# One decoder layer on one core: where the down product of five of eight expert waves stands

## The chip, the cores and the metric

The kernel runs on one core of a Trainium2 chip. The metric is the device time of one execution in microseconds (us). A run of the kernel before took 1399.57 us (median of three, 1397.91 to 1399.74). Tensor products run on TensorE (PE in the profile), elementwise work on VectorE (DVE), ScalarE (ACT) and GpSimd (POOL); SyncE (SP) issues the weight loads.

## The reference, cut to what matters

256 tokens of width 2048 pass one layer in float32: a convolution and an attention group, an output projection, a mixture of experts, and a gated layer embedding. What the change touches is the last two:

```
h = h + HierMoE(rms_norm(h))          # 32 experts, each token goes to two of them
    per expert e:  hidden = silu(xb @ w_gate[e]) * (xb @ w_up[e])     # 2048 -> 512, twice
                   y      = (hidden @ w_down[e]) * weight of the token  # 512 -> 2048
    out = sum of y by token
gate = sigmoid(rms_norm(h) @ w_ple_gate)                               # 2048 -> 2048
h = h + gate * (p @ w_ple)
```

The weights w_gate, w_up and w_down hold 32 x 2048 x 512 float32 each, 134 million bytes; all weights must be read once, 484 million bytes in all with inputs and outputs.

## The kernel before, in words

The order of all instructions on each engine is the order in which the program writes them. SBUF has 24 slots of 8 KB per partition (the tile tag "ring"), shared by the weight loads and the large buffers. The list `loads` fixes the order in which the weights are read; `pump` (L64) issues the next loads from it, on SP's queue (L74), whenever fewer than 24 slots less the reserved ones are in use, and `free` (L78) gives a slot back behind the instruction that read it last. Nearly every load is 1 MB, one slot.

The first stage (until about 385 us) makes the input projection, convolution, attention, output projection and routing. The 32 experts then run in eight waves of four, with 32 token slots an expert, so that a wave fills the 128 columns of the array's output side by side.

`gate_up(w)` (L949) multiplies the gathered tokens of a wave with its gate and up weights, 128 products of 512 columns in eight groups of four loads. After the third quarter it gathers the tokens of the next wave (`gather`, L933, products at L938). At its end it makes silu(gate) * up, transposes it (L990) and leaves it in SBUF (`hTw`). A gate or up load has 8 KB in one piece in HBM for each partition.

Only when all eight waves are through does the down product begin, by chunks of output columns (`TC`, L138): three of 512 columns and two of 256. For a chunk, `down_waves` (L1058) goes through the waves: `down_wave` (L1038, products at L1047) makes the outputs of a wave's four experts by slot in one PSUM bank, ScalarE copies them (L1064), and `scatter` (L1052, L1054) sums them by token, with the weights of the routing, into the tile `po`, which holds the chunk's sum of all waves for both halves of the tokens. `add_down` (L1070) adds it to the residual. A load of w_down is [128, 4, 512] or [128, 8, 256]: pieces of 2 KB or 1 KB.

Each finished chunk of columns is also a part of the contraction of the gate product. `gate_product(ci)` (L1138) runs in the background of the next chunk: every call of `bg` takes it one step on, and `down_waves` calls `bg` once behind each wave (`per=1`). Its first call transposes the chunk (`rows`, L1093), then each step splits a piece of gate weights in two parts (ScalarE L336, VectorE L337) and makes 12 products of 512 columns (L1128 to L1130). Of a 512 column chunk there are eight steps: four blocks of 512 output columns, two steps each; behind the second step of a block its two PSUM halves are copied or added to `gs` in SBUF (L1154 on ScalarE for chunk 0, L1156 on VectorE for later ones). The PSUM pool "pa" has two tiles of two banks: one holds `po` during a chunk, the other the block of the gate product. `drain` takes all steps that are left, ahead of the chunk's last wave. Of a 256 column chunk there are four steps, and their blocks alternate between a "pa" tile and two "ps" banks.

The loads follow the same order: gate and up of all waves, then for each chunk w_down of all waves and the chunk's gate weights. The last chunk ends with the norm's scale, the last gate steps, the sigmoid and the output.

Of the kernel before, what the change touches and what calls it, by code (L numbers as in the profile page):

```python
# [22 lines left out]
NW = NE // 4  # L23
NSLOT = 24
NEG_D = -1e30


@with_exitstack
def kernel(ctx: ExitStack, tc: tile.TileContext, I, out):
# [15 lines left out]

# [1 line left out]
    used, KEEP = [0], [0]  # L47

    def reserve(n):
        KEEP[0] += n  # L50
# [39 lines left out]

# [1 line left out]
    w_in_v = w_in.rearrange("(k p) n -> p k n", p=128)  # L92
# [39 lines left out]
    def want_d(w, c0, n):  # L132
        m = 512 // n
        for e in range(4 * w, 4 * w + 4, m):
            want(("d", e, c0), [128, 4 * m, n],
                 w_down[e:e + m].rearrange("e (j p) n -> p (e j) n", p=128)[:, :, c0:c0 + n])

    TC = [(0, 512), (512, 512), (1024, 512), (1536, 256), (1792, 256)]  # L138
    for w in range(NW):
        want_gu(w)  # L140
        if w == 5:
            want("p", [128, 2, 256], p.rearrange("(t p) k -> p t k", p=128))
            for k in range(2):
                want(("ple", k), [128, 2048], w_ple[128 * k:128 * k + 128, :])
    w_pg_v = w_pg.rearrange("(k p) n -> p k n", p=128)

    def pg_units(c0, cn):
        """first column and width of the loads of a chunk's gate weights"""
        if (c0, cn) == TC[-1]:
            return [(0, 512), (512, 512), (1024, 1024)]  # L150
        return [(n0, 2048 * 128 // cn) for n0 in range(0, D, 2048 * 128 // cn)]
# [8 lines left out]

    for c0, cn in TC[:3]:
        for w in range(NW):
            want_d(w, c0, cn)
        want_pgs(c0, cn)
    for c0, cn in TC[3:]:
        for w in range(NW):
            if w == NW - 1:
                want_pgs(c0, cn, 0)
            want_d(w, c0, cn)
        want_pgs(c0, cn, 1, 2) if cn == 256 else None  # L170

# [1 line left out]
    xs = [alloc([128, 4, 512], F32R, f"xs{i}") for i in range(4)]  # L173
# [47 lines left out]
    for s in range(2):  # L221
        nc.gpsimd.memset(onesbd[64 * s:64 * s + 64, 64 * s:64 * s + 64], 1.0)
    # a column of ones for each head
    hsel = kvt[:, 1920:2048]
    nc.gpsimd.memset(hsel, 0.0)
    for s in range(2):
        nc.gpsimd.memset(hsel[64 * s:64 * s + 64, s:128:18], 1.0)
    # -(distance) of a key from its query, far below zero outside the window
    nc.gpsimd.iota(dist[:, 0:128], pattern=[[1, 128]], base=0, channel_multiplier=-1,
# [26 lines left out]

# [2 lines left out]
    ss4 = C.tile([128, 2, 4], F32, name="ss4")  # L259
# [27 lines left out]
    def token_rows(pt, xrow, n):  # L287
        """adds a value by token to every row of pt"""
        for b in range(n):
            for tt in range(2):  # L290
                c0 = 256 * b + 128 * tt
                nc.tensor.matmul(pt[:, c0:c0 + 128], xrow[:, tt], ident, start=n == 1 and tt == 0,
                                 stop=b == n - 1 and tt == 1, skip_group_check=True)
# [32 lines left out]

# [1 line left out]
    granules = [("in", name, hf, q) for name, _, hf in units for q in range(2)]  # L328
# [24 lines left out]
    def keep_warm(n):  # L353
        """matmuls on constants, that the tensor engine's clock isn't gated while it waits"""
        for _ in range(n):
            nc.tensor.matmul(ps(), ident, wr.rearrange("p k n -> p (k n)")[:, 0:512], start=True, stop=True)
# [23 lines left out]

# [1 line left out]
    def halves(pt, dst):  # L382
# [38 lines left out]
    def q_sums(u):  # L421
        """sums of squares by token and head; the heads' scale goes on the scores"""
        sq = w2([128, 2, 256], "sq")
        q = qT[:, 2 * u:2 * u + 2, :]
        nc.gpsimd.tensor_mul(sq, q, q)
        yield
        yield
        if u == 0:
            prq[0] = ps()
        for b in range(2):  # L430
            h = 2 * u + b
            nc.tensor.matmul(prq[0][0:16, 0:256], hsel[:, 16 * h:16 * h + 16], sq[:, b],
                             start=h == 0, stop=h == 7)
        yield
        if u == 3:
            qs = w2([16, 256], "qs")
            nc.scalar.copy(qs, prq[0][0:16, 0:256])
            yield
            pv = ps()[:, 0:32].rearrange("p (t h) -> p t h", t=2)
            for tt in range(2):  # L440
                nc.tensor.transpose(pv[:, tt], qs[:, 128 * tt:128 * tt + 128], ident[0:16, 0:16])
            yield
            for tt in range(2):
                nc.scalar.activation(rq[:, tt], pv[:, tt], AF.Sqrt, bias=epsn[:, tt:tt + 1], scale=1.0 / HD)
            nc.vector.reciprocal(rq, rq)
            nc.vector.tensor_mul(rq, rq, slope[:, 1, None, :].to_broadcast([128, 2, NH]))
# [107 lines left out]
    def mixed(kb, y, sacc, gcol, eng):  # L554
        """two blocks of a head group's output: their squares, and their parts for the projection"""
        sq = w2([128, 2, 256], "sq")
# [56 lines left out]

# [1 line left out]
    rac = C.tile([128, 2, 2], F32, name="rac")  # L615
# [19 lines left out]
    def last_group(i, pt):  # L635
        """the last two granules: the first 128 tokens before the second, and those in two halves of the
        columns, so that the router's work on a part runs beside the products of the next"""
        hT = w2([128, 4, 128], "hT"), w2([128, 4, 128], "hT")
# [185 lines left out]

# [1 line left out]
    rt = C.tile([128, 2, 8], F32, name="rt")  # L826
# [12 lines left out]

    # the group: the first of the largest logits  # L840
    nc.vector.tensor_reduce(gm, Lg, axis=AX.X, op=OP.max)
# [3 lines left out]
    for tt in range(2):  # L845
# [4 lines left out]
                            gt[:, :, 12:16, None].to_broadcast([128, 2, NG, EPG]), op=OP.add)  # L850
    # its two experts: those above the second largest logit, then the first of those equal to it
    for tt in range(2):
# [16 lines left out]
    nc.tensor.matmul(pr2[:, 0:32], tri[:, 0], asg[:, 1], start=False, stop=True)  # L869
    # rank of a token among those of its expert, from 1 on; 0 where it isn't assigned  # L870
    for tt, pp in ((0, pr_), (1, pr2)):
# [14 lines left out]

    # assignments past an expert's slots, for the general path at the end
    cnt = C.tile([128, 32], F32, name="cnt")
# [12 lines left out]

# [1 line left out]
    xg, sel = {}, {}  # L903
# [45 lines left out]
    def gate_up(w):  # L949
# [4 lines left out]
        for j4 in range(4):  # L954
            if j4 == 0 and w == NW - 1:
                reserve(6)
            for n, nm in enumerate("gu"):
# [33 lines left out]
        nc.scalar.copy(hTw(w), p2)  # L991

    ple = [None, None]

# [26 lines left out]
    for w in range(NW):  # L1021
        gate_up(w)
        if w == 1:
            overflow_counts()
        if w == 4:
            reserve(3)
        if w == 5:
            ple_product()

# [1 line left out]
    acc = hmid  # L1031
    gs = [alloc([128, D], F32, "gs") for _ in range(2)]
    wsl[:] = [alloc([128, 2048], F32R, f"wsq{i}") for i in range(3)]
# [4 lines left out]
    def down_wave(w, c0, cn):  # L1038
        """the outputs of a wave's experts, by slot"""
        m = 512 // cn  # L1040
# [11 lines left out]
    def scatter(po, w, y, off, cn):  # L1052
        for tt in range(2):
            nc.tensor.matmul(po[:, tt, off:off + cn], swT(w)[:, 128 * tt:128 * tt + 128], y,  # L1054
                             start=w == 0 and (tt == 0 or cn == 512 or ci < last),
                             stop=w == NW - 1, skip_group_check=True)
# [36 lines left out]
    def rows(ci):  # L1093
        """the columns of a chunk, transposed, with the norm's gain, split in two parts"""
        c0, cn = TC[ci]
# [64 lines left out]
    for ci in range(last):  # L1160
        po = pa()
        prev = down_waves(po, range(NW - 1), *TC[ci], 0)
        drain()
# [9 lines left out]
    po = ps().rearrange("p (t n) -> p t n", t=2)  # L1173
    prev = down_waves(po, range(NW - 2), c0, cn, 0)
    drain()
# [55 lines left out]

# [1 line left out]
    def overflow():  # L1233
# [126 lines left out]
```

## Time and profile before

| | |
|---|---|
| runs, median (lowest, highest) | 1399.57 us (1397.91, 1399.74) |
| profiled execution: span | 1398.5 us, 1.07 us below the median of the runs |
| TensorE products (PE) busy | 1160.8 us, 83% |
| VectorE, ScalarE, POOL busy | 360.3, 265.2, 133.1 us |
| granted clock, mean | 0.937 |
| moved | 484.32 MB, mean 346 GB/s |
| chain that ended last | DMA 49%, PE 37%, DVE 5%, ACT 3%, SP's queue 3% |

The profile has one execution. Busy times are unions, so matmuls that overlap count once, but a product that waits for the end of its group's loads counts as busy. The span in 40 slices has one slice per 35 us. "idle before <-X" says how long an engine stood idle and what ended it.

### The profile page before, as it was taken

Reading aid. Unit: us, or ns where it says so; the run is one execution under the profiler, and the core shown is the slowest. Engines: PE = TensorE matmul, PEld = TensorE weight load, DVE = VectorE, ACT = ScalarE, POOL = GpSimd, SP = SyncE. Lnnn points to the kernel's source line nnn. Section 1 sums busy time; section 2 is a strip of 40 time slices with the busy share of each in tenths; the row PEclk is TensorE's granted clock in tenths of the full one; section 3 lists DMA queues with packets and bytes.
Section 4 is the critical chain, followed back from the end, with each engine's and each line's share of the span. In section 5 each row is a group of like instructions: output and inputs, shape, how many; then the busy total and the mean of one; then the engine's idle time right before and its main releaser. Section 6 shows DMA issues by size and latency. Waiting matters only on the chain.

```text
span 1398.5 us, 15423 instructions
## 1 busy us (share of the span) xinstructions
PE 1160.8 (83%) x6411; PEld 644.8 (46%) x6412; DVE 360.3 (26%) x535; ACT 265.2 (19%) x456; POOL 133.1 (10%) x157
## 2 busy tenths in 40 slices
PE   7999999999996967778687887866686886996996
PEld 6878777888751513224151431511111441443654
DVE  5747887555300000101010000100000211212325
ACT  5435555443100000000000010000000211111213
POOL 2215566000000000000000000000000000000002
PEclk9999999999998999999999898998998997997999
DMA  8972247976899999999999999999999999999993
GB/s 241 344 246 86 66 147 251 337 224 229 316 410 422 421 421 421 421 421 421 422 421 421 419 421 421 420 422 406 387 387 387 365 387 378 359 387 354 357 350 138
DMA packets 181638, 484.32 MB, mean 346 GB/s; under 512 B 7940, under 2 KB 78012, under 8 KB 149564
## 3 DMA queue, kind: packets, MB, share of 16 engines
q1 hardware_dynamic: 180572, 480.59, 90.6%
q0 software_dynamic: 992, 2.69, 0.6%
q8 instruction: 52, 0.85, 0.2%
q14 instruction: 22, 0.18, 0.0%
HBM read 478.80 MB, written 4.19 MB: 345 GB/s over the span
## 4 chain that ended last, share of the span: by engine, by line
DMA 49%; PE 37%; DVE 5%; ACT 3%; SPq 3%; issue 1%; POOL 1%; DVEq 0%; ACTq 0%
DMA ld<-in_w_up_dram 36%; DMA ld<-in_w_down_dram 12%; PE pst L1047 6%; PE pat L758 5%; PE pst L938 3%; SPq L74 3%; PE pat L759 3%; PE pat L963 3%; PE pat L736 2%; PE pat L738 2%; PE pat L737 2%; PE pat L1054 2%; PE pat L1129 1%; PE pat L1130 1%; PE pat L1128 1%
## 5 line engine op out<-in xcount | busy, mean ns | idle before, releaser
L963 PE MATMUL pat<-ld,xg 128*32 128x512 f32 x2048 | 340.7, 675 | 117.5 <-DMA ld<-in_w_up_dram 69.8
L963 PEld LDWEIGHTS pat<-ld,xg 128*32 128x32 f32 x2048 | 79.9, 120 | 363.9 <-issue 147.4
L1047 PE MATMUL pst<-ld,wv 128*32 128x512 f32 (+1 forms) x1280 | 169.4, 551 | 58.0 <-DMA ld<-in_w_down_dram 57.9
L758 PE MATMUL pat<-xs,wsp 128*128 128x512 f32 x544 | 196.3, 404 | 0.0
L759 PE MATMUL pat<-xs,wsp 128*128 128x256 f32 x544 | 153.1, 281 | 0.7 <-DVE wsp L337 0.7
L337 DVE TENSOR_TENSOR wsp<-ld,wsp 128x1024 fp32r<-128x1024 f32 x91 | 131.2, 1447 | 82.9 <-ACT wsp L336 82.9
L940 DVE TENSOR_TENSOR xg<-pst,gffn 128x512 f32<-128x512 f32 (+1 forms) x33 | 22.3, 675 | 438.4 <-PE pst L938 438.4
L336 ACT CAST wsp<-ld 128x1024 fp32r<-128x1024 f32 x104 | 108.0, 1049 | 91.7 <-PE pat L738 44.0
L1047 PEld LDWEIGHTS pst<-ld,wv 128*32 128x32 f32 x1280 | 45.6, 115 | 171.3 <-issue 87.5
L938 PEld LDWEIGHTS pst<-sel,x 128*128 128x128 f32 x512 | 112.6, 311 | 9.8 <-issue 8.1
L758 PEld LDWEIGHTS pat<-xs,wsp 128*128 128x128 f32 x544 | 103.2, 190 | 27.9 <-issue 2.8
L938 PE MATMUL pst<-sel,x 128*128 128x128 f32 x512 | 114.7, 384 | 0.0
L759 PEld LDWEIGHTS pat<-xs,wsp 128*128 128x128 f32 x544 | 103.7, 191 | 1.3 <-DVE wsp L337 1.3
L947 ACT COPY wv<-pst 128x256 f32<-128x256 f32 x8 | 3.0, 374 | 440.9 <-PE pst L946 440.9
L1064 ACT COPY y<-pst 128x512 f32<-128x512 f32 (+1 forms) x40 | 20.0, 501 | 306.6 <-PE pst L1047 306.6
L337 DVE TENSOR_TENSOR wsq<-ld,wsq 128x1024 fp32r<-128x1024 f32 x32 | 39.1, 1224 | 136.5 <-ACT wsq L336 136.5
L1128 PE MATMUL pat<-wsq,hs 128*128 128x512 f32 x112 | 53.4, 476 | 12.9 <-ACT wsq L336 11.8
L1054 PE MATMUL pat<-y,wv 128*128 128x512 f32 (+1 forms) x128 | 55.6, 562 | 0.0
L336 POOL CAST wsq<-ld 128x1024 fp32r<-128x1024 f32 x1 | 1.0, 1042 | 558.2 <-DVE x L1072 558.2
L736 PE MATMUL pat<-wsp,mx 128*128 128x512 f32 (+1 forms) x128 | 49.8, 389 | 0.1
L738 PE MATMUL pat<-wsp,mx 128*128 128x512 f32 (+1 forms) x128 | 49.0, 383 | 0.0
L931 POOL TENSOR_TENSOR sel<-sel,et 128x128 f32<-128x128 f32 x16 | 6.1, 400 | 451.3 <-DVE sel L929 357.5
(269 smaller groups left out, 1005.5 us busy)
## 6 DMA issues: line engine op xcount, KB each, us to landing
ld<-in_w_gate_dram SPq DMA_DIRECT2D x128, 1024.0 KB, 19.8
ld<-in_w_up_dram SPq DMA_DIRECT2D x128, 1024.0 KB, 19.8
ld<-in_w_down_dram SPq DMA_DIRECT2D x128, 1024.0 KB, 14.1
ld<-in_w_in_dram SPq DMA_DIRECT2D x35, 1024.0 KB, 12.6
ld<-in_w_out_dram SPq DMA_DIRECT2D x16, 1024.0 KB, 10.7
ld<-in_w_ple_gate_dram SPq DMA_DIRECT2D x15, 1024.0 KB, 14.3
x<-in_x_dram SPq DMA_DIRECT2D x8, 256.0 KB, 6.7
spill<-x POOLq DMA_DIRECT2D x8, 256.0 KB, 5.9
```

The costliest lines, as they stand in the source:

```text
L74: nc.sync.dma_start(t[:, i] if isinstance(src, list) else t, part)
L336: copy(t[:, :, 0], src)
L337: eng.tensor_sub(t[:, :, 1], src, t[:, :, 0].bitcast(F32))
L736: nc.tensor.matmul(o, mh, ws[:, kk, 0, cs], start=first, stop=False)
L738: nc.tensor.matmul(o, ml, ws[:, kk, 0, cs], start=False, stop=last)
L758: nc.tensor.matmul(pt[:, b, :], ws[:, kk, 0, bs], xk, start=first, stop=False)
L759: nc.tensor.matmul(pt[:, b, 0:256], ws[:, kk, 1, bs], xk[:, 0:256], start=False, stop=last)
L938: nc.tensor.matmul(pt[:, 128 * jj:128 * jj + 128], hmid[tt][:, j::16], sel[w][:, tt], start=tt == 0, stop=tt == 1)
L963: nc.tensor.matmul(pt[32 * e:32 * e + 32, n, :], g[:, j, 32 * e:32 * e + 32], wt, start=j == 0, stop=j == 15, tile_position=(0, 32 * e))
L1047: nc.tensor.matmul(pt[32 * e:32 * e + 32, 0:cn], hv[:, j, 32 * e:32 * e + 32], d, start=j == 0, stop=j == 3, tile_position=(0, 32 * e))
L1054: nc.tensor.matmul(po[:, tt, off:off + cn], swT(w)[:, 128 * tt:128 * tt + 128], y, start=w == 0 and (tt == 0 or cn == 512 or ci < last), s ...
L1128: nc.tensor.matmul(pt[tt], mh, ws[:, kk, 0], start=start and b == 0, stop=False)
```

## The change

A constant `NROW = 5` is added. For waves 0 to 4 the loads of w_down move from the chunks to the place behind the wave's gate and up loads, and are whole rows, [128, 2048], 16 of 1 MB per wave. A new function `down_rows` runs directly behind `gate_up` for these waves: 64 products into four PSUM banks, four copies, eight scatter products, and eight additions (for the first wave copies) on VectorE into two new SBUF buffers `macc`, which hold the sum by token. Behind the last wave the two sums are added to the residual, and the buffers become `gs`. The chunks keep waves 5 to 7; `bg` is called three times behind each of waves 5 and 6 (in the last chunk twice behind wave 5). A few reservations of slots change with the two buffers; comment lines are dropped.

```diff
+NROW = 5
@@
+    def want_rows(w):
+        for j in range(4):
+            for e in range(4 * w, 4 * w + 4):
+                want(("r", e, j), [128, D], w_down[e, 128 * j:128 * j + 128, :])
@@
     for w in range(NW):
         want_gu(w)
+        if w < NROW:
+            want_rows(w)
@@
     for c0, cn in TC[:3]:
-        for w in range(NW):
+        for w in range(NROW, NW):
             want_d(w, c0, cn)
         want_pgs(c0, cn)
     for c0, cn in TC[3:]:
-        for w in range(NW):
+        for w in range(NROW, NW):
@@ gate_up
             if j4 == 0 and w == NW - 1:
-                reserve(6)
+                reserve(4)
@@
+    macc = [None, None]
+
+    def down_rows(w):
+
+        hv = hTw(w).rearrange("p (j s) -> p j s", j=4)
+        pts = [ps() for _ in range(4)]
+        for j in range(4):
+            for n in range(4):
+                for e in range(4):
+                    nc.tensor.matmul(pts[n][32 * e:32 * e + 32, :], hv[:, j, 32 * e:32 * e + 32],
+                                     arrived["r", 4 * w + e, j][:, 512 * n:512 * n + 512],
+                                     start=j == 0, stop=j == 3, tile_position=(0, 32 * e))
+            free(4)
+        ys = []
+        for n in range(4):
+            y = w2([128, 512], "y")
+            nc.scalar.copy(y, pts[n])
+            ys.append(y)
+        for n in range(4):
+            ns = slice(512 * n, 512 * n + 512)
+            po = pa()
+            for tt in range(2):
+                nc.tensor.matmul(po[:, tt], swT(w)[:, 128 * tt:128 * tt + 128], ys[n], start=True, stop=True)
+            for tt in range(2):
+                if w == 0:
+                    if n == 0:
+                        macc[tt] = alloc([128, D], F32, "macc")
+                    nc.vector.tensor_copy(macc[tt][:, ns], po[:, tt])
+                else:
+                    nc.vector.tensor_add(macc[tt][:, ns], po[:, tt], macc[tt][:, ns])
@@
     for w in range(NW):
         gate_up(w)
+        if w == 0:
+            reserve(2)
+        if w < NROW:
+            down_rows(w)
+        if w == 3:
+            free()
@@
     acc = hmid
-    gs = [alloc([128, D], F32, "gs") for _ in range(2)]
+    for tt in range(2):
+        nc.vector.tensor_add(acc[tt], acc[tt], macc[tt])
+    gs = macc
@@ scatter
-                             start=w == 0 and (tt == 0 or cn == 512 or ci < last),
+                             start=w == NROW and (tt == 0 or cn == 512 or ci < last),
@@
-        prev = down_waves(po, range(NW - 1), *TC[ci], 0)
+        prev = down_waves(po, range(NROW, NW - 1), *TC[ci], 0, per=3)
@@
-    prev = down_waves(po, range(NW - 2), c0, cn, 0)
+    prev = down_waves(po, range(NROW, NW - 2), c0, cn, 0, per=2)
```

## Rows read from the trace of the kernel before

**Rows 1.** The span in 40 slices: TensorE in tenths, and transfer rate.
```profile
PE   7999999999996967778687887866686886996996
GB/s 241 344 246 86 66 147 251 337 224 229 316 410 422 421 421 421 421 421 421 422 421 421 419 421 421 420 422 406 387 387 387 365 387 378 359 387 354 357 350 138
```

**Rows 2.** Busy us (x instructions) by window; last: granted clock, DMA share, GB/s.
```profile
560.00:960.00 400.00, 300.78 (x1632) 120.21 (x1635) 24.00 (x52) 13.03 (x25) 3.04 (x8) 0.92 1.01 421
788.00:812.00 24.00, 22.08 (x132) 16.20 (x130) 3.82 (x6) 0.97 (x2) 0.00 (x0) 1.00 1.01 418
980.00:1066.00 86.00, 61.15 (x282) 15.16 (x274) 1.29 (x2) 4.69 (x8) 0.00 (x0) 0.96 1.05 387
1286.00:1355.00 69.00, 68.05 (x580) 45.33 (x582) 24.74 (x32) 15.66 (x28) 0.00 (x0) 1.00 1.10 353
```

**Rows 3.** The chain that ended last: start us, us, what.
```profile
788.69 14.17 PE pst L938 x64
...
949.13 19.84 DMA ld<-in_w_up_dram
...
1355.62 12.47 DMA ld<-in_w_down_dram
1368.13 1.92 PE pst L1047 x16
```

**Rows 4.** TensorE's timeline, second chunk: start us, us, line, operation, count.
```profile
1077.32 5.43 PE L1047 MATMUL pst<-ld,wv 128*32 128x512 f32 x26 [0.79 <-DMA ld<-in_w_down_dram]
1082.68 1.09 PE L1104 MATMUL pst<-ident,x 128*128 128x128 f32 x8
1087.76 0.76 PE L1128 MATMUL pat<-wsq,hs 128*128 128x512 f32 x1 [3.99 <-ACT wsq L336]
1089.02 0.79 PE L1129 MATMUL pat<-wsq,hs 128*128 128x512 f32 x1 [0.50 <-DVE wsq L337]
...
1094.01 3.93 PE L1047 MATMUL pst<-ld,wv 128*32 128x512 f32 x32
...
1102.56 3.64 PE L1047 MATMUL pst<-ld,wv 128*32 128x512 f32 x32
...
1110.80 3.64 PE L1047 MATMUL pst<-ld,wv 128*32 128x512 f32 x32
```

**Rows 5.** Timeline, the evacuations of the gate product's blocks on ScalarE and VectorE.
```profile
1102.66 1.07 ACT L1154 COPY gs<-pat 128x512 f32<-128x512 f32 x2 [3.06 <-PE pat L1130]
...
1254.80 1.29 DVE L1156 TENSOR_TENSOR gs<-pat,gs 128x512 f32<-128x512 f32 x2 [4.61 <-PE pat L1130]
```

**Rows 6.** TensorE's timeline, end of the third chunk.
```profile
1254.14 0.39 PE L1129 MATMUL pat<-wsq,hs 128*128 128x512 f32 x1
1254.37 0.39 PE L1130 MATMUL pat<-wsq,hs 128*128 128x512 f32 x1
1254.69 3.64 PE L1047 MATMUL pst<-ld,wv 128*32 128x512 f32 x32
1258.26 3.70 PE L1054 MATMUL pat<-y,wv 128*128 128x512 f32 x8
```

**Rows 7.** TensorE's timeline, the last chunk of 256 columns.
```profile
1327.71 1.93 PE L1047 MATMUL pst<-ld,wv 128*32 128x256 f32 x32
...
1334.15 1.93 PE L1047 MATMUL pst<-ld,wv 128*32 128x256 f32 x32
...
1339.84 1.93 PE L1047 MATMUL pst<-ld,wv 128*32 128x256 f32 x32
1345.53 1.93 PE L1047 MATMUL pst<-ld,wv 128*32 128x256 f32 x32
...
1357.57 3.60 PE L1182 MATMUL pat<-gs,ident 128*128 128x512 f32 x8
1361.10 1.93 PE L1047 MATMUL pst<-ld,wv 128*32 128x256 f32 x32
1362.96 1.99 PE L1054 MATMUL pst<-y,wv 128*128 128x256 f32 x8
```

## The prediction

> **What bounds the kernel now.** I read three views in this order: the span in slices, the busy time by window, and the chain of waits. The slices [rows 1] show two regimes behind the first quarter: slices at about 421 GB/s while gate and up weights are read, then about 387 and 350 GB/s while w_down is read, with TensorE between 6 and 9 tenths busy. The windows [rows 2] give the rates: 421 GB/s in 560 to 960 us, 387 in 980 to 1066 us (chunks of 512 columns), 353 in 1286 to 1355 us (chunks of 256). So a load of 1 MB (1.0486 million bytes) takes 2.49, 2.71 and 2.97 us. The chain [rows 3] names transfers nearly everywhere: the last of w_up lands at 968.97, and the last w_down tile at 1368.1, which TensorE consumes at once (until 1370.05). From there to the end of the span are 28.4 us of norm, gate and output, on which the change does not touch. One stretch differs: in 1286 to 1355 us TensorE is busy 68.05 of 69 us [rows 2]. There the two are level.
>
> I work against the profiled execution, whose span is 1398.5 us; the median of the runs shown is 1399.57, so 1.1 us lie around the span. I add my difference to the median.
>
> **What the change moves.** 80 tiles of w_down (5 waves x 16) leave the column chunks and are read as whole rows between the gate and up loads. The new order is: eight waves of gate and up with five waves of rows in between, then for each chunk three waves of w_down and the chunk's gate weights.
>
> Step 1, the rows' transfers. Gate and up tiles have 8 KB in one piece per partition and so have the rows. w_ple, two whole-row tiles of this very shape, is read inside 788 to 812 us, where the rate is 418 [rows 2]. So I price a row tile at 2.49 us: 80 x 2.49 = +199 us in the expert stage. The other end is the 2.71 us of a w_down tile today, 18 us more in all. I take 2.49, by the row of the same shape. SP issues as many loads as before (16 a wave in either form), and POOL's queue none.
>
> Step 2, the expert stage stays bound by transfers. A wave then holds 48 loads, 119 us. TensorE is busy 300.78 of 400 us today [rows 2], 60 us per 80 us wave, part of that waiting. The rows add 4 x 3.6 us of products, four pairs of scatter matmuls (half of 3.70 us each, [rows 6]), and two short waits, on the copy of the hidden values and of y: about 24 us. 84 is below 119. The ring keeps about 16 load slots (two go to the sums by token), 40 us of loads; the longest stretch in which TensorE frees none is the gathering of the next wave's tokens, 14.2 us [rows 3], already there today. The new adds on VectorE (8 a wave, 0.65 us each, as in [rows 5]) and the final addition of the sums to the residual run beside transfers: no cost. If that cover were gone, it would be some 5 us a wave.
>
> Step 3, when TensorE can begin the second chunk. Today the first wave of chunk 1 begins on its last tiles at 1077.32 [rows 4]. Five waves fewer in chunk 0 give back 20 x 2.71 = 54 us, the rows cost 199: now 1077.3 - 54.2 + 199.0 = 1222.1. It cannot be earlier, since that is transfers end to end. The gate product of chunk 0 stands in the program behind that wave's products, so TensorE has nothing to do with its idle time before.
>
> Step 4, transfers from there on. Chunk 1 holds 16 tiles, 43 us, and so does chunk 2; the two narrow chunks some 23 us each. Alone they would finish at about 1345, 23 us before today: 60 x (2.71 - 2.49) + 20 x (2.97 - 2.49) = 23. That is what the change can give.
>
> Step 5, TensorE from there on. The down products shrink to three eighths, but the gate product of each chunk stays whole: 8 steps of 12 matmuls. In today's steady cycle down, scatter and one step take 1102.56 to 1110.80 = 8.2 us [rows 4]; steps follow each other at 0.23 us a matmul, 2.8 us each [rows 6]. A chunk begins with a break: transposes, VectorE, ScalarE and the first split weights, 1082.68 to 1089.02, 6.1 us without its first matmul, 3.99 us of it TensorE idle [rows 4].
>
> Today each step is followed by a wave's down product. Now three steps run in a row (two waves, then two steps in the drain). A column block is two steps, and its PSUM tile is one of two of that pool, of which the chunk's own sum holds the other. So the next block must wait until both halves are evacuated. That takes 1.07 us on ScalarE in chunk 0 and 1.29 us on VectorE in the others, and both start only after the last matmul of the block (1254.80 against its start at 1254.37) [rows 5]. Today the next down product covers this. With the way to and back it is 1.2 and 1.5 us, three times a chunk. Behind it stands everything on TensorE: the next steps, the next wave's down product, and the slots that these free. No row shows TensorE in that wait; its ends are 0 and 1.5, and I take the upper, since only one tile is free.
>
> The sum, in us:
> - Chunk 1: first wave and first step as today 1077.32 to 1094.01 = 16.7; two steps and a wait 6.8; second wave 8.2 + 1.2 + 5.6 = 15.0; drain 1.2 + 5.6 = 6.8; third wave with both scatters 1254.69 to 1261.96 = 7.3 [rows 6]. Together 52.6.
> - Chunk 2: down 3.6, break 6.1, three steps and a wait 9.9; 15.3; 7.1; 7.3. Together 49.3.
> - Chunk 3 (256 columns): 1.9 + 6.1 + 9.9; 5.7 + 7.1 (the cycle is 1339.84 to 1345.53, [rows 7]); 7.1; 3.9. Together 41.7.
> - Chunk 4: wave, break and step 1327.71 to 1334.15 = 6.4; three steps 8.4; four preloads 3.5; down and scatters 1361.10 to 1364.95 = 3.9; last down 1.9 [rows 7]. Together 24.1.
>
> That is 167.7: the last down product ends at 1222.1 + 167.7 = 1389.8 instead of 1370.05. The 28.4 us behind it stay. **So +19.8 us: 1399.6 + 19.8 = 1419 us.** Transfers, 23 us early, would wait for slots: the stage has turned from transfer to TensorE.
>
> The clock is a second open term. After waits on transfers the matmuls of the first step go at half rate, 11 in 1089.02 to 1094.01, 0.45 us each [rows 4], against 0.23; I count that in chunk 1 alone, where TensorE still waits for transfers. The Trainium skill (TensorE: Matmul & The Clock Gate, "Why this matters for your kernels") says that idle gaps between bursts send the engine back to half its clock; by it the breaks of chunks 2 and 3 would also be followed by a slow step. In this trace the clock is 1.00 over the whole dense stretch of 1286 to 1355 us [rows 2], which holds one short break only, so it settles neither.
>
> **Rivals.**
> 1. Half rate (1.2 in place of 2.4 GHz) after each break. For it: today's break in chunk 1 is followed by it. Against it: today TensorE waited for loads before that break. Two breaks, one to two steps each at 12 x 0.2 = 2.4 us: 5 to 10 us more, about 1426. The skill's rule above is this case.
> 2. No wait for evacuation, because the tile's halves are released one by one, or early enough. Then 3.6 + 4.5 + 4.5 = 12.6 us fall away: 1407. For it: no row shows the wait. Against: both evacuations start together and late [rows 5].
> 3. The other side, faster: the last transfer still sets the end. Its place is chunks 1 to 4; it decides once TensorE needs less than 43 us per full chunk. The gain is then the 23 us of step 4: 1377. For it: nearly the whole chain today is transfers. Against: today's cycle of 8.2 us is measured with everything loaded, eight steps alone are 22.4 us, three waves 15, the break 6; with no evacuation wait and no slow first step at all the sum still gives 1403.
> 4. The change does not do what it says: rows are read no quicker than chunks, or the ring runs dry behind the rows' products. 18 us more: 1437. Against it stands w_ple's stretch at 418.
>
> **How the numbers follow.** Forecast 0.50, at 1413 to 1424; rival 1 0.17; rival 2 0.16; rival 3 0.08; rival 4 0.04; the rest 0.05, spread around no change. What a measurement tells from no change is 0.2%, 2.8 us. Slower: 0.50 + 0.17 + 0.04 and nearly all of rival 2, with some of the rest: 0.86. Same: 0.04. Faster: 0.10, rival 3 and some of the rest. The range, 1402 to 1430, holds the forecast and rivals 1 and 2, whose lowest sum is 1403.
>
> **What would show it.** Slices at 421 GB/s until about 1168 us, then three waves at 387, then, from about 1230 us, rates well under 387 with TensorE at 9 tenths. The first matmul of a gate step (L1128) would show idle time put down to the evacuation of the sums (ScalarE in the first chunk's product, VectorE in later ones), nine times 1.2 to 1.5 us; if it doesn't, rival 2 holds. Slow steps behind the breaks of chunks 2 and 3 show rival 1. If TensorE's idle time in the last 170 us is mostly put down to w_down's transfers, step 5 is wrong and rival 3 holds; and if the last gate and up tile lands well off 1168, steps 1 and 2 are.

## The result, and the profile after

The changed kernel takes 1420.85 us (median of four runs, 1420.42 to 1422.14) against 1399.65 us before; the ratio is 1.0154, with an interval of 1.0141 to 1.0167. So it is 21.2 us slower; 19.8 us slower was forecast. The profiled execution has a span of 1420.2 us, 21.7 us more than before.

The span in 40 slices after the change, TensorE in tenths and the transfer rate, answers to [rows 1]; a slice is 35.5 us:

```profile
PE   7999999999988787687758768687978667697896
GB/s 246 344 228 91 69 166 239 339 204 262 319 420 422 421 421 421 421 421 421 422 420 422 421 421 422 422 420 422 419 421 422 422 413 387 377 286 377 297 92 61
```

The 421 GB/s now last until slice 32, five and a half slices longer than before. Behind them stand only three slices near 387 (387, 377 and 377); between and behind these the rate falls to 286, 297 and 92, although weights are read until about 1369 us. By windows (busy us and counts of PE, PEld, DVE, ACT, POOL; last the granted clock, the DMA share and GB/s), answering to [rows 2]:

```profile
600.00:1160.00 560.00, 426.02 (x2208) 159.56 (x2212) 41.01 (x78) 20.06 (x37) 3.02 (x8) 0.91 1.01 421
1222.00:1369.00 147.00, 124.57 (x666) 77.30 (x666) 52.39 (x61) 42.24 (x62) 0.00 (x0) 0.93 0.88 306
```

The expert stage runs at 421 GB/s with the rows in it, so a row tile does cost 2.49 us. From 1222 us until the last load is in, at about 1369 us, the transfers fill 0.88 of the engines' time where [rows 2] had 1.05 and 1.10: they wait. What SP's queue waits for in 1222 to 1400 us (us in total, times, longest) are slots, which the splits of gate weights and the down products give back:

```profile
SPq L75 <- DVE wsq L345: 59.9, 11, 10.0
SPq L75 <- PE pst L1094: 33.9, 7, 8.0
```

TensorE's timeline from the end of the expert stage on (start us, us, line, operation, count; in brackets the idle time before it and what ended it), answering to [rows 4] and [rows 7]. L971 is the gate and up product, L1094 the chunks' down product, L1151 the transposes, L1175 to L1177 a gate step:

```profile
1168.02 5.32 PE L971 MATMUL pat<-ld,xg 128*32 128x512 f32 x26 [1.51 <-DMA ld<-in_w_up_dram]
...
1222.63 5.35 PE L1094 MATMUL pst<-ld,wv 128*32 128x512 f32 x26 [0.79 <-DMA ld<-in_w_down_dram]
1227.91 1.09 PE L1151 MATMUL pst<-ident,x 128*128 128x128 f32 x8
1233.00 0.80 PE L1175 MATMUL pat<-wsq,hs 128*128 128x512 f32 x1 [3.99 <-ACT wsq L344]
...
1274.29 3.64 PE L1094 MATMUL pst<-ld,wv 128*32 128x512 f32 x32
...
1282.88 0.51 PE L1175 MATMUL pat<-wsq,hs 128*128 128x512 f32 x1 [3.92 <-ACT wsq L344]
...
1285.14 0.63 PE L1175 MATMUL pat<-wsq,hs 128*128 128x512 f32 x1
1285.57 0.63 PE L1176 MATMUL pat<-wsq,hs 128*128 128x512 f32 x1
...
1287.66 0.39 PE L1175 MATMUL pat<-wsq,hs 128*128 128x512 f32 x1
1287.89 0.39 PE L1176 MATMUL pat<-wsq,hs 128*128 128x512 f32 x1
...
1323.71 1.93 PE L1094 MATMUL pst<-ld,wv 128*32 128x256 f32 x32
...
1366.41 1.93 PE L1094 MATMUL pst<-ld,wv 128*32 128x256 f32 x32
...
1388.20 2.82 PE L1094 MATMUL pst<-ld,wv 128*32 128x256 f32 x32
```

The last gate and up tile comes at 1168.02, the first product of chunk 1 on its last tile at 1222.63 (1222.1 was forecast). It is the last product there that waits for a load: chunks 2, 3 and 4 begin at 1274.29, 1323.71 and 1366.41 with nothing in brackets. The last down product ends at 1391, and 29.2 us later the span.

Who waited for whom on TensorE in 1168 to 1400 us (us in total, times, longest):

```profile
PE pst L1094 <- DMA ld<-in_w_down_dram: 16.9, 9, 6.4
PE pat L1175 <- ACT wsq L344: 11.8, 3, 4.0
PE pat L1175 <- DVE macc L1203: 5.9, 4, 1.5
...
PE pat L1175 <- ACT macc L1201: 2.3, 2, 1.2
PE pat L1176 <- DVE wsq L345: 1.9, 4, 0.8
```

The 16.9 us for loads all lie in chunk 0 and the start of chunk 1. The three breaks give 11.8 us. The evacuation waits that the trace of before did not show are there, 1.16 us each behind ScalarE and 1.47 behind VectorE, but six, not nine.

### The profile page after: what moved, and what is told of

The parts are those of the page before. It is cut to its first block, busy times and chain, and to the rows that moved or that the text cites. A ratio compares the mean times of both kernels' runs of the same rounds, so it can differ in the third digit from the quotient of the medians.

```text
span 1420.2 us, 15126 instructions
## 1 busy us (share of the span) xinstructions
PE 1170.3 (82%) x6231; PEld 637.9 (45%) x6232; DVE 389.1 (27%) x577; ACT 265.4 (19%) x451; POOL 133.0 (9%) x157
## 4 chain that ended last, share of the span: by engine, by line
DMA 54%; PE 32%; DVE 6%; ACT 3%; SPq 1%; issue 1%; POOL 1%; DVEq 0%; ACTq 0%
DMA ld<-in_w_up_dram 27%; DMA ld<-in_w_down_dram 17%; DMA ld<-in_w_gate_dram 10%; PE pat L766 5%; PE pst L1094 3%; PE pat L767 3%; PE pat L971 3%; PE pst L946 2%; PE pat L744 2%; PE pat L746 2%; PE pat L1176 2%; PE pat L745 2%; PE pat L1175 2%; PE pat L1177 2%; PE pat L1101 1%
## 5 line engine op out<-in xcount | busy, mean ns | idle before, releaser
L971 PE MATMUL pat<-ld,xg 128*32 128x512 f32 x2048 | 339.6, 669 | 120.3 <-DMA ld<-in_w_up_dram 73.5
L971 PEld LDWEIGHTS pat<-ld,xg 128*32 128x32 f32 x2048 | 77.9, 120 | 370.3 <-issue 145.3
L1010 PE MATMUL pst<-ld,wv 128*32 128x512 f32 x640 | 119.9, 734 | 41.3 <-DMA ld<-in_w_down_dram 37.9
L1010 PEld LDWEIGHTS pst<-ld,wv 128*32 128x32 f32 x640 | 26.8, 129 | 131.1 <-DMA ld<-in_w_down_dram 71.5
L1094 PE MATMUL pst<-ld,wv 128*32 128x512 f32 (+1 forms) x480 | 61.0, 556 | 16.9 <-DMA ld<-in_w_down_dram 16.9
L1175 PE MATMUL pat<-wsq,hs 128*128 128x512 f32 x112 | 48.3, 432 | 21.1 <-ACT wsq L344 11.8
L1030 DVE TENSOR_TENSOR macc<-pat,macc 128x512 f32<-128x512 f32 x32 | 20.6, 686 | 156.3 <-PE pat L1023 155.9
L345 DVE TENSOR_TENSOR wsq<-ld,wsq 128x1024 fp32r<-128x1024 f32 x32 | 38.6, 1222 | 42.1 <-ACT wsq L344 41.2
L744 PE MATMUL pat<-wsp,mx 128*128 128x512 f32 (+1 forms) x128 | 49.8, 389 | 0.1
L746 PE MATMUL pat<-wsp,mx 128*128 128x512 f32 (+1 forms) x128 | 49.0, 383 | 0.0
L745 PE MATMUL pat<-wsp,mx 128*128 128x512 f32 (+1 forms) x128 | 49.0, 383 | 0.0
## 6 DMA issues: line engine op xcount, KB each, us to landing
ld<-in_w_gate_dram SPq DMA_DIRECT2D x128, 1024.0 KB, 19.8
ld<-in_w_up_dram SPq DMA_DIRECT2D x128, 1024.0 KB, 19.8
ld<-in_w_down_dram SPq DMA_DIRECT2D x128, 1024.0 KB, 19.8
```

The costliest lines, as they stand in the source:

```text
L345: eng.tensor_sub(t[:, :, 1], src, t[:, :, 0].bitcast(F32))
L744: nc.tensor.matmul(o, mh, ws[:, kk, 0, cs], start=first, stop=False)
L745: nc.tensor.matmul(o, mh, ws[:, kk, 1, cs], start=False, stop=False)
L746: nc.tensor.matmul(o, ml, ws[:, kk, 0, cs], start=False, stop=last)
L971: nc.tensor.matmul(pt[32 * e:32 * e + 32, n, :], g[:, j, 32 * e:32 * e + 32], wt, start=j == 0, stop=j == 15, tile_position=(0, 32 * e))
L1010: nc.tensor.matmul(pts[n][32 * e:32 * e + 32, :], hv[:, j, 32 * e:32 * e + 32], arrived["r", 4 * w + e, j][:, 512 * n:512 * n + 512], star ...
```

## The experiments

My theory: from 1222 us on TensorE's own work, in the order in which the program puts it, sets the end; the transfers would be some 23 us earlier. The rivals: the new order of loads or the fewer free slots set the end; or the rows themselves cost something.

**Less TensorE work, in both kernels.** The edit, in the kernel before and in the changed one:

```diff
+                if ci < last:
+                    nc.tensor.matmul(pt[tt], mh, ws[:, kk, 0], start=start and b == 0, stop=b == kn - 1)
+                    continue
```

> The kernel before, with the gate product's background steps (all but the last chunk's) cut to one of their three matmuls per block; the low parts of tokens and weights are left out of the product, while every load, split and evacuation stays. Theory (before, the last transfer sets the end): TensorE gives up 28 steps x 8 x 0.23 = 51 us of work and the time falls by less than 8 us, to 1392 to 1400. Rival (before, TensorE already set the end in the chunks): it falls by 20 us or more.

Measured: 1396.72 us, ratio 0.9981 (0.9971 to 0.9991).

> The changed kernel with the same cut: one of three matmuls in the gate product's background steps, all loads, splits and evacuations kept. Theory (behind 1222 us TensorE's own work sets the end): a full chunk needs about 33 us of TensorE instead of 49, less than its 43 us of transfers, so the end falls back to the last transfer, 1376 to 1384 us, and the difference to the first run shows the transfers' gain of some 20 us. Rival (the new order of loads, or fewer free slots, sets the end): it stays above 1410.

Measured: 1384.34 us, ratio to before 0.9894 (0.9877 to 0.991). Two windows of each, columns as above, first the kernel before with the cut:

```profile
1220.00:1340.00 120.00, 90.29 (x620) 42.37 (x614) 35.67 (x45) 24.69 (x42) 0.00 (x0) 0.89 1.08 363
1340.00:1360.00 20.00, 16.06 (x128) 7.83 (x121) 1.29 (x2) 1.12 (x3) 0.00 (x0) 0.91 1.10 350
```

and the changed kernel with the cut:

```profile
1220.00:1340.00 120.00, 92.37 (x486) 43.69 (x486) 54.23 (x65) 44.99 (x70) 0.00 (x0) 0.86 1.06 373
1340.00:1360.00 20.00, 18.04 (x109) 9.73 (x108) 10.12 (x17) 5.03 (x9) 1.04 (x1) 1.00 0.04 17
```

The same cut takes 2.6 us from the kernel before and 36.5 us from the changed one: before, transfers set the end; after, TensorE does. With the cut the loads run at 1.06 of the engines' time again, so neither their order nor the slots held them. They are through at about 1341 us (17 GB/s in the 20 us from 1340 on), while those of the kernel before with the cut go on until about 1365. That is the transfers' gain, 24 us where 23 were forecast. Of it only 12.4 us reach the end (20 were expected): the last down product still comes at 1351, behind the last chunks' splits and evacuations, ten us after the last load.

**The evacuation waits.** Every second block goes to the other PSUM pool:

```diff
-                pt = two(kq == 1 and n % 2)
+                pt = two(n % 2)
```

> The changed kernel; every second column block of the gate product goes to two single banks of the other PSUM pool, so that a block need not wait until the one before it is evacuated. Theory (six waits of 1.2 to 1.5 us stand in TensorE's path): 8 us less, 1411 to 1415, and no idle time before a step put down to the evacuation. Rival (the waits only hide another limit, the splits or the loads): less than 2 us.

Measured: 1413.42 us, ratio 1.0101 (1.0084 to 1.0118), 7.4 us less than the changed kernel. Who waited for whom on TensorE, 1168 to 1400 us:

```profile
PE pst L1094 <- DMA ld<-in_w_down_dram: 18.4, 10, 6.4
PE pat L1175 <- ACT wsq L344: 11.8, 3, 4.0
...
PE pat L1176 <- DVE wsq L345: 1.6, 4, 0.5
```

Both rows of `macc` are gone, 8.2 us, and the time follows by 7.4: the waits stood in the path.

**The break.** The gate product's first call ends behind the transposes, so that the next wave's down product stands in the 4 us of the break:

```diff
         squares(ci)
+        yield
         kq = TC[ci][1] // 256
@@ down_waves
-            for _ in range(per):
+            for _ in range(1 if w == NROW else per):
@@
-        prev = down_waves(po, range(NROW, NW - 1), *TC[ci], 0, per=3)
+        prev = down_waves(po, range(NROW, NW - 1), *TC[ci], 0, per=4)
```

> The changed kernel; the gate product's first call ends behind the transposes of the chunk, and its eight steps follow behind the second wave's down product, which so stands in the break of 4 us. Theory: each of chunks 1 to 3 loses part of its break (2.6, 5.6 and 2.5 us by my sums, with one more evacuation wait each), about 10 us in all: 1406 to 1415. Rival (the break is covered by something else that is late): no change, or slower by the added waits.

Measured: 1419.94 us, ratio 1.0151 (1.0134 to 1.0168): no gain to speak of, a miss. The waits on TensorE, same stretch:

```profile
PE pst L1094 <- DMA ld<-in_w_down_dram: 21.3, 13, 6.4
PE pat L1175 <- DVE macc L1204: 8.8, 6, 1.5
PE pat L1175 <- ACT macc L1202: 3.5, 3, 1.2
```

Of the breaks' 11.8 us all but 1.0 are gone, but nine evacuation waits instead of six give back 4.1 us, and waits for loads 4.4 us. The chain shows the latter (start us, us, what):

```profile
1266.14 3.69 PE pst L1094 x32
1269.83 0.26 SPq L75
...
1271.28 11.67 DMA ld<-in_w_down_dram
...
1282.99 5.22 PE pst L1094 x26
```

and TensorE's timeline the wave that waits:

```profile
1277.87 1.05 PE L1094 MATMUL pst<-ld,wv 128*32 128x512 f32 x4
```

The load that chunk 2's second wave waits for was issued at 1271 only, when the down product of chunk 1's last wave had given back its slots. The second wave came forward into the break, from 1293.88 to 1277.87 us, and its loads did not. The wave then takes until 1288.15, 10.3 us with 3.0 us idle, against 3.6 us in the changed kernel: part of the waiting counts as busy, and much of what was left of the gain goes there. I had priced the break, and not when the loads are issued for the wave that fills it. That it is the gate weights, whose steps now all stand behind that wave, that kept the slots is my reading; no run tried it apart.

**Fewer waves of rows.** `NROW` is 3 or 4, two or three gate steps behind each wave. With three, the chunks still read the hidden values of the first four waves, so these keep one slot more.

> The changed kernel with three waves of rows in place of five, five waves in the chunks, two gate steps behind each. Theory: in the full chunks TensorE then needs 60 us against 65 us of transfers, so transfers set the pace again and only the narrow chunks lag; the first product of chunk 1 on its last loads comes at 1165, the last down product ends at 1366, 4 us before today's kernel before: 1393 to 1399. Rival (rows themselves cost, in the expert stage or by the two slots of the sums): it lies at three fifths of the change's loss, 1412.

Measured: 1406.82 us, ratio 1.0054 (1.004 to 1.0068), a miss by 8 us.

> The changed kernel with four waves of rows, four in the chunks, three gate steps behind each. Theory: 55.6 us of TensorE against 54.2 of transfers in the first full chunk, a lag that grows from there; two evacuation waits fewer a chunk; the last down product ends at 1374: 1400 to 1408. Rival (rows themselves cost): four fifths of the loss, 1416.

Measured: 1406.53 us, ratio 1.0049 (1.0035 to 1.0063), as expected.

With three rows I had set 65 us of transfers against 60 us of TensorE in a full chunk and taken the larger. The windows of that run show neither:

```profile
1160.00:1180.00 20.00, 14.11 (x49) 6.57 (x50) 6.35 (x7) 5.99 (x10) 0.00 (x0) 0.67 1.03 381
1180.00:1200.00 20.00, 20.00 (x112) 10.62 (x112) 3.20 (x3) 7.02 (x10) 0.00 (x0) 0.99 0.74 268
...
1220.00:1240.00 20.00, 14.38 (x45) 3.35 (x44) 1.29 (x2) 0.58 (x2) 0.00 (x0) 0.74 1.05 381
1240.00:1260.00 20.00, 15.32 (x75) 9.25 (x74) 9.72 (x11) 7.90 (x13) 0.00 (x0) 0.91 0.83 306
```

In the break and the slow step behind it TensorE frees nothing, and some 15 us later the transfers drop to 268 GB/s (SP's queue waits for the down product's slots, as the wait rows of three rows alone show below). At the next chunk TensorE waits for the loads that were not asked for then. So the first full chunk takes 70.1 us, 1163.36 to 1233.49, more than the larger of the two. The slots (eleven by the program's count, 24 less 13 that are held here) seem too few for either side to run ahead of the other's pause; no run changed their number alone. That is 5 us of the nearly 11 by which the last down product, ending at 1376.7 us, is late against the 1366 that I had worked out: the second full chunk takes 64.7 us, and behind 1298.19 us TensorE waits for no load. The rest lies in the narrow chunks, where TensorE's own work sets the pace and the breaks stand in its path.

**Fewer rows with both edits.** Three and two waves of rows, with alternate PSUM pools and the filled break:

> Three waves of rows, every second block of the gate product in the other PSUM pool, and the break behind the transposes filled with the next wave's down product (three gate steps behind each later wave). Theory: the full chunks are set by transfers, so only chunk 3's break counts: 3 to 6 us less than three rows alone, 1388 to 1395. Rival (as with five rows, the later gate steps keep slots and turn the break into waits for loads): the same as three rows alone.

Measured: 1391.7 us, ratio 0.9944 (0.993 to 0.9957).

> The same with two waves of rows, two gate steps behind each later wave. Theory: all full chunks wait for transfers (76 us against 65 of TensorE), narrow ones lag a little: within 3 us of three rows, 1389 to 1396. Rival (each wave of rows gains its transfers' part, some 4.6 us, wherever): 4 to 6 us slower than three rows.

Measured: 1391.25 us, ratio 0.9942 (0.9928 to 0.9955). Both beat the kernel before as well as the changed one. SP's queue in 1160 to 1300 us, who waited for whom, first three rows alone:

```profile
SPq L75 <- PE pst L1092: 50.4, 9, 12.5
```

then three rows with both edits:

```profile
SPq L75 <- PE pst L1092: 38.8, 11, 8.7
```

and two windows of the latter:

```profile
1180.00:1200.00 20.00, 19.43 (x97) 12.77 (x96) 5.81 (x5) 9.80 (x14) 0.00 (x0) 1.00 1.02 370
...
1240.00:1260.00 20.00, 20.00 (x109) 11.12 (x102) 6.82 (x7) 6.81 (x11) 0.00 (x0) 1.00 1.05 387
```

Where three rows alone had 268 and 306 GB/s, there are now 370 and 387: TensorE frees slots through the break. The full chunks take 65.9 and 60.8 us, 8.2 us less together; nearly all the rest of the 15.1 us is gained in the narrow chunks, 6.5 us, where three rows alone left TensorE a break and a slow step. The two runs differ also in when the steps are called (two or three behind a wave), and neither this nor the two edits were tried apart with three rows.

**Is it the rows or the order of the steps?**

> The kernel before, without any rows, with the two edits of the last two runs alone: alternate PSUM pools for the gate product's blocks, and the break filled with the next wave's down product. Theory (before, transfers set the pace but in chunk 3, whose break is in TensorE's path): 3 to 7 us less than before, 1392 to 1397, so that rows are worth 1 to 5 us on top. Rival (the whole gain of the two-row and three-row runs is the order of the gate steps): 1391.

Measured: 1398.12 us, ratio 0.9988 (0.9979 to 0.9997), a miss by 1 us: in the kernel before, the edits are nearly worthless, since there TensorE waits for loads anyway. Waits on TensorE in 1000 to 1385 us, first the kernel before:

```profile
PE pst L1047 <- DMA ld<-in_w_down_dram: 50.3, 28, 6.5
PE pat L1128 <- ACT wsq L336: 11.8, 3, 4.0
```

then with the edits, where the second row is gone and the first has grown:

```profile
PE pst L1047 <- DMA ld<-in_w_down_dram: 57.4, 37, 6.3
```

> The changed kernel, five waves of rows, with both edits. Theory (with the break filled alone, 12.3 us of evacuation waits stood in TensorE's path): these fall away, 1405 to 1411, still slower than before, since TensorE needs more per chunk than its 43 us of transfers. Rival (loads held back by kept slots set the end there): 1416 or more.

Measured: 1405.79 us, ratio 1.0046 (1.0033 to 1.006), as expected: with five rows the transfers stay idle for a part of the time even so (0.88 in the window), and they are through at about 1355 us, while the last down product begins at 1372:

```profile
1240.00:1280.00 40.00, 35.50 (x180) 20.75 (x182) 13.59 (x14) 15.58 (x24) 0.00 (x0) 1.00 0.88 321
```

> One wave of rows with both edits, seven waves in the chunks, two gate steps behind each later wave. Theory: transfers set the pace, each wave of rows is worth up to 4.6 us until TensorE lags: 1391 to 1396, between no rows and two. Rival (rows give nothing): as with no rows.

Measured: 1393.36 us, ratio 0.9951 (0.9937 to 0.9964). With both edits the ratios by waves of rows are thus 0.9988, 0.9951, 0.9942, 0.9944 and 1.0046 for none, one, two, three and five. The first wave brings 0.4%, 5 us, about the 4.6 us that its transfers save; from two on nothing is gained, and five lose.

## Why the prediction was right

**Steps 1 to 3, transfers and the start of chunk 1.** Right. The last gate and up tile moved from 969.0 to 1168.0, by the 199.0 us of 80 row tiles at 2.49 us; the rate in the stage is 421 GB/s. TensorE was never the limit there, and the additions on VectorE (0.69 us each; the final ones 2.28 us each, at 1175) cost nothing.

**Step 4, the transfers' gain of 23 us.** Right, but out of reach: it shows once TensorE's work is cut, with the last load at about 1341 us (about 1345 was forecast).

**Step 5, TensorE's sum.** 167.7 us were forecast from the start of chunk 1 to the end of the last down product; 1222.63 to 1391.0 are 168.4. By chunks: 51.7, 49.4, 42.7 and 24.6 us against 52.6, 49.3, 41.7 and 24.1. The small difference hides three terms that were mis-sized and cancel; a fourth stands behind it:
- The evacuation waits are six, not nine, 8.2 us instead of 12.6: 4.4 us less. Each chunk's first pair of blocks has none. The timeline of the changed kernel, chunk 1 (columns as above), shows the copies beside the next block's matmuls, and the later wait:

```profile
1242.39 1.07 ACT L1201 COPY macc<-pat 128x512 f32<-128x512 f32 x2 [4.94 <-PE pat L1177]
...
1242.64 0.39 PE L1177 MATMUL pat<-wsq,hs 128*128 128x512 f32 x1
1242.87 0.39 PE L1175 MATMUL pat<-wsq,hs 128*128 128x512 f32 x1
...
1253.36 1.07 ACT L1201 COPY macc<-pat 128x512 f32<-128x512 f32 x2 [3.04 <-PE pat L1177]
...
1254.48 0.50 PE L1175 MATMUL pat<-wsq,hs 128*128 128x512 f32 x1 [1.16 <-ACT macc L1201]
```

  I had both PSUM tiles taken from the chunk's start; the chunk's sum is first written behind the second wave's product, and until then a second tile is free. The run with the break filled bears this out: there the second wave's product stands ahead of all steps, and all nine waits are there.
- The slow step behind the breaks of chunks 2 and 3, my first rival, is real but shorter: the matmuls start 0.43 us apart from 1284.1 on, behind 3.92 us in which TensorE stood idle, and 0.23 us apart from 1287.66 on, 1.7 us lost instead of 2.4 to 5. Twice, 3.4 us. Windows of the changed kernel around that break (columns as above) show the granted clock at 1.00, 0.51 (the 1.2 GHz level) and 1.00 (2.4 GHz):

```profile
1278.00:1282.00 4.00, 0.96 (x8) 0.72 (x7) 2.08 (x4) 1.95 (x4) 0.00 (x0) 1.00 1.05 387
1284.10:1287.60 3.50, 3.46 (x8) 2.79 (x9) 2.36 (x2) 1.84 (x2) 0.00 (x0) 0.51 1.05 386
1287.70:1296.00 8.30, 8.30 (x48) 5.52 (x50) 2.42 (x3) 1.05 (x1) 0.00 (x0) 1.00 1.05 387
```

  The Trainium skill's rule (TensorE: Matmul & The Clock Gate, "Why this matters for your kernels"), that idle gaps between bursts send the engine back to half its clock, agrees with this.
- The last wave's down product in a narrow chunk takes 2.75 us, not 1.9, since its experts go two at a time there (the 2.82 us of 1388.20): 1.7 us in two chunks.
- What follows the last down product takes 29.2 us instead of 28.4.

With the start 0.5 us late: 19.8 + 0.5 - 4.4 + 3.4 + 1.7 + 0.8 = 21.8, against 21.7 us in the spans. So the mechanism was right, and that the sum came within 2 us was partly luck.

**The rivals.** No wait for evacuation (1407): fell, though a third of the waits is not there; alternate pools bring 7.4 us. The last transfer sets the end (1377): fell with the cut of TensorE's work. Rows that are no quicker, or a ring that runs dry behind the rows' products (1437): fell; 421 GB/s throughout. Half rate behind each break (1426): part of it is there, 3.4 us of 5 to 10. What the prediction left out, and only the misses of the later runs brought up, is that the slots tie both sides together: with five rows TensorE, which waits for no load behind the start of chunk 1, was so far behind that it did not matter.

## What to carry to other kernels

Moving work forward to where an engine has idle time takes it from where it covered something: here the down products of five waves had separated the gate steps, covered their evacuations and given TensorE's other work the time of their loads. Before such a move, work out for the stage that stays behind how long each of its limits takes alone; five waves left 43 us of transfers beside 49 us of TensorE per chunk, and one to three waves of rows, with the steps put apart, were enough. Where two limits are near to each other, the buffers between them count as well: price what a pause of the one keeps from being issued on the other, not just the larger of both.

## What the runs showed of the hardware

Loads of 1 MB run at 421 GB/s in pieces of 8 KB per partition, at 387 in pieces of 2 KB and at about 350 in pieces of 1 KB (with a few loads of gate weights in pieces of 4 KB among them), each with the engines' time filled (shares of 1.01, 1.05 and 1.10 in the windows). It was not expected that the engines count as fuller where they move less.
